# Queries and first-pair keys split once for both heads in a hybrid attention layer

## The chip, the cores and the metric

The kernel runs on one core of a Trainium2 chip. Its engines are TensorE (PE: matmuls and transposes), VectorE (DVE), ScalarE (ACT), GpSimd (POOL) and SyncE (SP), whose queue issues nearly all transfers. The metric is the device time of one execution in microseconds, the median of several runs.

## The reference

One layer over 1024 tokens of width 1024 in float32. It projects the normalised input once, and two mixers share the columns: a dilated sliding-window attention with 8 heads of 64, and a gated linear recurrence (HGRN2) with 4 heads of 128. An output projection and a squared-ReLU MLP follow.

```python
h = rmsnorm(x, mix_pre_norm[layer])
proj = h @ w_in[layer]
q_a, k_a, v_a, q_h, f_h, i_h, g_h = jnp.split(proj, splits, axis=-1)
attn = dilated_mixture_attention(q_a, k_a, v_a, slopes)   # (128,1), (512,4), (2048,16)
attn = rmsnorm(attn.reshape(B, S, ATTN_WIDTH), attn_out_norm[layer])
rec = hgrn2_recurrence(q_h, f_h, i_h, g_h, lower_bounds[layer], hgrn_out_norm[layer])
mixed = jnp.concatenate([attn, rec], axis=-1) @ w_out[layer]
x = x + rmsnorm(mixed, mix_post_norm[layer])
h = rmsnorm(x, mlp_pre_norm[layer])
ff = jnp.square(jax.nn.relu(h @ w_ff1[layer])) @ w_ff2[layer]
x = x + rmsnorm(ff, mlp_post_norm[layer])
```

In each branch of the attention the scores are `q k / 8` plus a bias that falls with distance; the three branches are combined by their softmax denominators.

## The kernel before, in words

**Precision.** A matmul in `float32r` keeps only part of a float32. So the kernel splits an operand into a high part (a copy that rounds, on ACT) and a low part (the difference, on DVE or POOL) and multiplies in three passes (`three_pass`, L89 to L92).

**Stages.** The heads of the recurrence come first: `hgrn_core(h)` for h = 0 to 3, each with projections of the next head as a filler on PE. During the core of the last head (h = 3) the filler is `attn_proj(0)` and `attn_proj(1)`, the projections of the first two pairs of attention heads. In that core each of seven levels multiplies `kt` and `qt` on DVE (L597, L599), makes the products `pl` of the next level on PE (L593) and merges them by a mask (L604). Then follow 64 steps of attention, eight per head (`s = 8 * hd + i`), with `attn_proj(2)`, `attn_proj(3)` and the first part of the output projection (`early_out`, its matmuls write `pwe`) as fillers. Then the rest of the output projection and the MLP, which are dense on PE.

**What sets the order.** The order is written out by hand and each engine takes its instructions in that order. `fill(ns)` lets the filler's generators issue a few matmuls; in a step, `UNITS[hd][i]` fills are shared between its first and its second half. `hooks[s]` is called between the two halves. `wo_half(k, c)` scales and splits half a block of the output weights (ACT L140, DVE L141), `row_turn(t, 0)` transposes four blocks of a row of the recurrence's result (PE L1174) and splits them into `emt` (ACT L86, DVE L87).

**Queries.** `attn_proj(pr)` projects a pair of heads at a time: partitions 0 to 63 of the result are the first head and 64 to 127 the second. For each half of the tokens DVE reads the bank with the factor -0.125 and the row's norm (L796) into the staging tile `qf`, in which the tokens stand by class (token mod 4). The matmul for the scores contracts over 128 partitions: a head's stack holds the query's high part in its own 64 partitions and the low part in the other 64, against keys whose high parts (`kh`) and low parts (`kl`) stand twice. So for each head ACT copies the high part into its place (L801) and POOL subtracts (L802) into the tile `ql`; SP then sends the low parts across (L803, L804).

**Keys.** `keys_read` (L731) reads a half of the keys into `kf`; `key_job` (L742) does one head of it: ACT L753, POOL L754, and two transfers (L757) to the other 64 partitions. For the first pair both jobs come at once, for later pairs one in each of several steps.

**Scores.** `look` multiplies queries and keys (PE L893, L894), and DVE adds the bias and takes the smallest value in one instruction (L898); the signs are turned, so that the smallest is the softmax's maximum. The bias tables are made by `table_part` on POOL (L718, L720) ahead of the attention. `raise_` is the exponential (ACT L951), `turn` transposes its result (`pt_D`, `pt_F`, `pt_N`: PE L961, L973, L970).

The staging tiles `half` have two buffers, which `qf`, `ql`, `kf` and the values' `vf` take in turn.

Of the kernel before, what the change touches and what calls it, by code (L numbers as in the profile page):

```python
# [9 lines left out]
F32R = mybir.dt.float32r  # L10
U8 = mybir.dt.uint8
AF = mybir.ActivationFunctionType
ALU = mybir.AluOpType
# [4 lines left out]
P = 128  # L18
# [10 lines left out]
DIL = 4  # L29
FAR = 192  # L30


def f32(ap):
    return ap.bitcast(F32)
# [3 lines left out]
def hymba_layer(ctx, tc, x, w_in, w_out, w_ff1, w_ff2, g_pre, lb_logits, g_mix, g_post,  # L38
# [21 lines left out]
    def half(name, dtype=F32):  # L60
        return sp.tile([P, 512], dtype, tag="half", name=name, bufs=2)
# [133 lines left out]
    def fill(ns, least=False):  # L195
        debt[0] += ns
        if least:
            debt[0] = max(debt[0], 1.0)
        while debt[0] > 0 and queue:
            try:  # L200
                cost = next(queue[0])
            except StopIteration:
                queue.pop(0)
                continue
            if cost is None:
                break
            debt[0] -= cost
        debt[0] = min(debt[0], 0.0)
# [191 lines left out]
    def in_blocks(ap):  # L400
        return ap.rearrange("p (j i r) -> p j r i", i=32, r=DIL)

    def classes(ap):
        return ap.rearrange("p (m r) -> p r m", r=DIL)

    def by_class(ap):
        return ap.rearrange("p (j r i) -> p j r i", i=32, r=DIL)
# [285 lines left out]
    def table_part():  # L693
        n = table_box["next"]
        hd, part_ = divmod(n, 2)
        if n > 2 * AH:
            return
        table_box["next"] += 1
        if part_ == 0 and hd > 0:
            nc.sync.dma_start(out=table_dram[hd - 1], in_=table_box["out"][:, :NEAR + FAR])  # L700
        if hd == AH:
            return
        if n == 0:
            table_box["raw"] = slab("S", "traw")
            G.memset(table_box["raw"][:, :FAR * DIL], -1.0e30)
        if part_ == 0:
            table_box["out"] = slab("S", f"tout{hd}")
        raw, dst = table_box["raw"], table_box["out"]
        w = NEAR // 2
        near_cols = bias_tab[hd][:, T - NEAR + part_ * w:T - NEAR + (part_ + 1) * w].rearrange("(i r) c -> r i c", r=DIL)  # L710
        for r in range(DIL):
            nc.sync.dma_start(out=raw[32 * r:32 * r + 32, FAR * DIL:], in_=near_cols[r])
        if part_ == 0:
            for b in range(4, NT):
                n = (b - 1) * P
                nc.sync.dma_start(out=raw[(b - 4) * 32:(b - 3) * 32, :n],
                                  in_=bias_tab[hd].rearrange("(i r) c -> i r c", r=DIL)[:, 0, 896 - b * P:896 - b * P + n])
        G.tensor_scalar(by_class(dst[:, part_ * w:(part_ + 1) * w]), in_blocks(raw[:, FAR * DIL:]), -1.0, None, op0=ALU.mult)  # L718
        if part_ == 0:
            G.tensor_scalar(dst[:, NEAR:NEAR + FAR],  # L720
                            raw[:, :FAR * DIL].rearrange("p (k r) -> p k r", r=DIL)[:, :, 0], -1.0, None, op0=ALU.mult)

    first_done = [False] * (AH // 2)
    A0 = 4 * HH
# [3 lines left out]
    turn_later = []  # L728
    second_done = [False] * (AH // 2)

    def keys_read(pr, pm, hf):  # L731
        sl = slice(hf * 512, hf * 512 + 512)
        full = half(f"kf{pr}{hf}")
        V.tensor_tensor(out=full.rearrange("p (r m) -> p r m", r=DIL), in0=classes(pm),
                        in1=rrow[:, sl].rearrange("p (r m) -> p r m", r=DIL), op=ALU.mult)
        key_jobs.extend((pr, i, hf, full) for i in range(2))
        keys_done[pr] += 1
        if pr == 0:
            key_job()
            key_job()  # L740

    def key_job():  # L742
        if not key_jobs:
            return
        pr, i, hf, full = key_jobs.pop(0)
        a, b = halves[i]

        def place_of(t):
            return t.rearrange("p (r m) -> p r m", r=DIL)[:, :, hf * P:(hf + 1) * P]
        st = pairs[pr][0][i]  # L750
        kh, kl = place_of(st["kh"]), place_of(st["kl"])
        src = full.rearrange("p (r m) -> p r m", r=DIL)[a:b]
        S.activation(kh[a:b], src, AF.Copy)  # L753
        G.tensor_tensor(out=kl[a:b], in0=src, in1=f32(kh[a:b]), op=ALU.subtract)  # L754
        c, d = halves[1 - i]
        for t in (kh, kl):
            nc.sync.dma_start(out=f32(t[c:d]), in_=f32(t[a:b]))  # L757
# [17 lines left out]
    def attn_proj(pr):  # L775
        stacks = [{}, {}]
        box = [None]
        while pr > 1 and not second_done[pr - 2]:
            yield None
        w = w_get(A0 + 3 * pr, 0)  # L780
        for hf in range(2):
            sl = slice(hf * 512, hf * 512 + 512)
            for n, cost in enumerate(proj_t(w, f"aq{pr}", hf, box)):
                if hf == 0 and n == 3 and turn_later:
                    values_turn()
                    cost += 450.0
                if hf == 0 and n == 4:
                    w_get(A0 + 3 * pr)
                if pr == 0 and hf == 0 and n == 5:
                    rrow_by_class(1)  # L790
                yield cost
            if hf == 0:
                for i in range(2):
                    stacks[i]["q"] = slab("S", f"q{pr}_{i}", F32R)
            full = half(f"qf{pr}{hf}")
            V.scalar_tensor_tensor(full.rearrange("p (r m) -> p r m", r=DIL), classes(box[0]), -0.125,  # L796
                                   rrow[:, sl].rearrange("p (r m) -> p r m", r=DIL), op0=ALU.mult, op1=ALU.mult)
            lo = half(f"ql{pr}{hf}", F32R)
            for i, (a, b) in enumerate(halves):
                src = full[a:b].rearrange("p (r j i) -> p j r i", r=DIL, i=32)  # L800
                S.activation(by_class(stacks[i]["q"][a:b, sl]), src, AF.Copy)  # L801
                G.tensor_tensor(out=by_class(lo[a:b]), in0=src, in1=by_class(f32(stacks[i]["q"][a:b, sl])), op=ALU.subtract)  # L802
            nc.sync.dma_start(out=f32(stacks[0]["q"][64:128, sl]), in_=f32(lo[0:64]))  # L803
            nc.sync.dma_start(out=f32(stacks[1]["q"][0:64, sl]), in_=f32(lo[64:128]))  # L804
            yield 650.0
        wv = w_get(A0 + 3 * pr + 1, 0)
        vs = None

        def values(hf):
            for n, cost in enumerate(proj_t(wv, f"av{pr}", hf, box)):  # L810
                if n == 4:
                    w_get(A0 + 3 * pr + 1 + hf)
                yield cost
            full = half(f"vf{pr}{hf}")
            V.tensor_tensor(out=by_class(full), in0=in_blocks(box[0]),
                            in1=rrow[:, hf * 512:hf * 512 + 512].rearrange("p (r j i) -> p j r i", r=DIL, i=32), op=ALU.mult)
            turn_later.append((pr, vs, full, hf))
            yield 650.0

        vs = slab("V8", f"v{pr}", F32R, (P, NT, 2, 2, 64))  # L820
        yield from values(0)
        while pr > 0 and not first_done[pr - 1]:
            yield None
        wk = w_get(A0 + 3 * pr + 2, 0)
        for i in range(2):
            stacks[i]["kh"] = slab("S", f"kh{pr}_{i}", F32R)
            stacks[i]["kl"] = slab("S", f"kl{pr}_{i}", F32R)
        pairs[pr] = (stacks, vs)
        for hf in range(2):
            for n, cost in enumerate(proj_t(wk, f"ak{pr}", hf, box)):  # L830
                if n == 3 and hf == 0:
                    values_turn()
                    cost += 450.0
                yield cost
            keys_read(pr, box[0], hf)
            if hf == 0 and pr == AH // 2 - 1:
                early_rows()
            yield 650.0
        yield from values(1)
# [29 lines left out]
    def look(hd, kind, g):  # L869
# [25 lines left out]
            got.append((dst, pS[:, o:o + n], bias, i))  # L895
            o += n
        for dst, src, bias, i in got:
            V.tensor_tensor_reduce(out=dst, in0=src, in1=bias, scale=1.0,  # L898
                                   scalar=3.0e38, op0=ALU.add, op1=ALU.min, accum_out=least[:, i:i + 1])

    def far_queries(hd):
# [398 lines left out]
    for h in range(HH):  # L1300
# [10 lines left out]
        1: lambda: last_gate(1),  # L1311
        2: lambda: last_gate(2),
        3: lambda: last_gate(3),
        43: lambda: wo_half(1, 0),
        45: lambda: wo_half(1, 1),
        46: lambda: [row_turn(0, 0, tag="s"), wo_half(2, 0)],
        47: lambda: [wo_half(2, 1), drain(), early_sums(), queue.extend(early_out(t) for t in range(NE))],
        48: lambda: [values_turn("t"), wo_half(3, 0)],
        49: lambda: load_bias(AH - 1),
        50: lambda: [wo_half(3, 1), row_turn(1, 0)],  # L1320
        52: lambda: row_turn(2, 0),
        54: lambda: row_turn(3, 0),
        55: lambda: [wo_half(4, 0), row_load(0)],
# [17 lines left out]
    for s in range(n_steps):  # L1341
# [46 lines left out]
        hooks.get(s, lambda: None)()  # L1388
        for _ in range(units - units // 2):
            fill(0.0, True)  # L1390
        if i in (1, 2):
            swap_low(hd, i - 1)
        if i == 7:
# [908 lines left out]
```

## Time and profile before

| | us |
|---|---|
| median of 3 runs | 1208.02 (1207.78 to 1208.76) |
| profiled execution, time | 1208.16 |
| profiled execution, span from the first to the last instruction | 1206.1 |
| PE busy | 1195.9 (99%) |
| DVE busy | 852.4 (71%) |
| ACT busy | 548.9 (46%) |
| POOL busy | 307.9 (26%) |

The granted clock of TensorE is 0.999. In the views below, a row of an engine's instructions in order of time has its start, its duration (both us), engine, line, operation, what it writes and reads, and the count of the instructions merged into it; in brackets stands the engine's idle time before it and what ended it. A row of waits has the total, the number and the longest of the waits. `xN: a/b/c` are the shortest, median and longest duration in ns. "DMA to landing" runs from an issue to the arrival of its data. PE's matmuls overlap and their ends are modelled.

### The profile page before, as it was taken

How to read it: one execution, taken by the hardware profiler on the slowest of the kernel's cores; microseconds unless marked ns; L12 is line 12 of the kernel's file. 1: busy time of each engine (PE TensorE's matmuls, PEld its weight loads, DVE VectorE, ACT ScalarE, POOL GpSimd, SP SyncE). 2: the span in 40 equal slices, each digit the busy share in tenths (PEclk: the TensorE clock that was granted, in tenths of full speed). 3: DMA queues.
4: the chain of work that ended last, by engine and by line, in shares of the span. 5: the costliest groups of instructions: out<-in, count | busy, mean ns of one | idle time of the engine just before them, and what ended most of it. 6: DMA issues, size and time to landing. Idle time of an engine off the chain costs nothing.

```text
span 1206.1 us, 17280 instructions
## 1 busy us (share of the span) xinstructions
PE 1195.9 (99%) x6342; PEld 1025.6 (85%) x6342; DVE 852.4 (71%) x1438; ACT 548.9 (46%) x1075; POOL 307.9 (26%) x290
## 2 busy tenths in 40 slices
PE   9999999999999999999999999999999999999998
PEld 8898989888888888888888888888888888888886
DVE  5696978776666768676689566766688553578796
ACT  7633333332565668755664222222234543434562
POOL 0121112021221210153321786575631000000022
PEclk9999999999999999999999999999999999999999
DMA  5222323123545456273514565554587534533337
GB/s 218 71 68 84 95 85 93 52 82 80 147 96 122 124 130 159 56 242 105 192 63 159 180 215 190 189 194 144 204 318 269 190 105 140 169 94 105 105 105 279
DMA packets 87091, 172.31 MB, mean 143 GB/s; under 512 B 14560, under 2 KB 40032, under 8 KB 87008
## 3 DMA queue, kind: packets, MB, share of 16 engines
q1 hardware_dynamic: 86864, 171.22, 44.3%
q8 instruction: 50, 0.82, 0.3%
q14 instruction: 33, 0.27, 0.1%
q10 hardware_dynamic: 144, 0.00, 0.0%
HBM read 116.91 MB, written 47.99 MB: 137 GB/s over the span
## 4 chain that ended last, share of the span: by engine, by line
PE 93%; DVE 2%; ACT 2%; issue 1%; DMA 0%; POOL 0%; DVEq 0%; POOLq 0%; ACTq 0%
PE f L2042 18%; PE f2s L2042 7%; PE pig L92 2%; PE pig L90 2%; PE pig L91 2%; PE pl L529 2%; PE pwo L90 2%; PE pwo L92 2%; PE pwo L91 2%; PE pm_ak L90 1%; PE pm_av L90 1%; PE pm_ak L92 1%; PE pm_ak L91 1%; PE pm_av L92 1%; PE pm_av L91 1%
## 5 line engine op out<-in xcount | busy, mean ns | idle before, releaser
L87 DVE TENSOR_TENSOR al<-ar,ah 128x1024 fp32r<-128x1024 f32 x56 | 70.6, 1260 | 80.5 <-ACT ah L86 78.2
L2042 PE MATMUL f<-bh,ah 128*128 128x512 f32 x320 | 124.5, 389 | 0.0
L2042 PE MATMUL f<-bl,ah 128*128 128x512 f32 x320 | 124.5, 389 | 0.0
L2042 PE MATMUL f<-bh,al 128*128 128x512 f32 x320 | 124.5, 389 | 0.0
L86 ACT ACTIVATE ah<-ar 128x1024 fp32r<-128x1024 f32 x56 | 59.1, 1056 | 86.9 <-DMA ar<-actd 83.3
L2042 PEld LDWEIGHTS f<-bh,ah 128*128 128x128 f32 x320 | 60.1, 188 | 12.6
L2042 PEld LDWEIGHTS f<-bh,al 128*128 128x128 f32 x320 | 60.1, 188 | 12.5
L2042 PEld LDWEIGHTS f<-bl,ah 128*128 128x128 f32 x320 | 60.1, 188 | 12.3
L2116 POOL TENSOR_SCALAR lbl<-ssq 128x1 f32<-128x1 f32 x4 | 3.3, 820 | 245.6 <-ACT fd L2112 245.5
L1665 POOL TENSOR_TENSOR e<-x,e 128x512 f32<-128x512 f32 x14 | 21.6, 1540 | 131.2 <-DVE x L1616 124.0
L2042 PE MATMUL f2s<-bl,ah 128*128 128x512 f32 (+1 forms) x128 | 48.9, 382 | 0.0
L2042 PE MATMUL f2s<-bh,al 128*128 128x512 f32 (+1 forms) x128 | 48.9, 382 | 0.0
L2042 PE MATMUL f2s<-bh,ah 128*128 128x512 f32 (+1 forms) x128 | 48.9, 382 | 0.0
L718 POOL TENSOR_SCALAR tout<-traw 128x256 f32<-128x256 f32 x16 | 18.4, 1149 | 109.2 <-DMA traw<-in_bias_tab_dram 93.4
L754 POOL TENSOR_TENSOR kl<-kf,kh 64x512 fp32r<-64x512 f32 x16 | 21.3, 1329 | 86.3 <-ACT kh L753 55.6
L87 DVE TENSOR_TENSOR bl<-br,bh 128x1024 fp32r<-128x1024 f32 x32 | 40.1, 1252 | 1.1 <-ACT bh L86 0.9
L2059 ACT ACTIVATE acc<-f 128x512 f32<-128x512 f32 x28 | 16.8, 598 | 49.6 <-PE f L2042 49.6
L802 POOL TENSOR_TENSOR ql<-qf,q 64x512 fp32r<-64x512 f32 x16 | 21.3, 1334 | 62.6 <-ACT q L801 62.0
L86 ACT ACTIVATE bh<-br 128x1024 fp32r<-128x1024 f32 x32 | 33.6, 1051 | 4.4 <-PE f L2042 3.1
L87 DVE TENSOR_TENSOR wl<-raw,wh 128x1024 fp32r<-128x1024 f32 x21 | 25.9, 1233 | 9.3 <-ACT wh L86 9.3
L90 PE MATMUL pwo<-woh,mt 128*128 128x512 f32 x80 | 32.2, 402 | 0.0
L92 PE MATMUL pwo<-woh,mt 128*128 128x512 f32 x80 | 31.3, 391 | 0.0
(1722 smaller groups left out, 3964.2 us busy)
## 6 DMA issues: line engine op xcount, KB each, us to landing
ar<-actd SPq DMA_DIRECT2D x56, 512.0 KB, 3.7
br<-in_w_ff_dram SPq DMA_DIRECT2D x16, 1024.0 KB, 6.2
raw<-in_w_in_dram SPq DMA_DIRECT2D x28, 512.0 KB, 4.0
w1r<-in_w_ff_dram SPq DMA_DIRECT2D x14, 1024.0 KB, 6.5
actd<-e SPq DMA_DIRECT2D x17, 768.0 KB, 4.3
actd<-e SPq DMA_DIRECT2D x11, 1024.0 KB, 4.1
xr<-in_x_dram SPq DMA_DIRECT2D x8, 512.0 KB, 8.3
raw<-in_w_out_dram SPq DMA_DIRECT2D x8, 512.0 KB, 3.6
```

The lines of the kernel that those rows point to most:

```text
L86: S.activation(hi, src, AF.Copy)
L87: eng.tensor_tensor(out=lo, in0=src, in1=f32(hi), op=ALU.subtract)
L90: TE.matmul(dst, lhs[0], rhs[0], start=start, stop=False)
L91: TE.matmul(dst, lhs[0], rhs[1], start=False, stop=False)
L92: TE.matmul(dst, lhs[1], rhs[0], start=False, stop=stop)
L529: TE.matmul(pl[:, n % 2, :192], kt[:, n * P:(n + 1) * P], sets[u // 2][:, n % 4], start=True, stop=True)
L718: G.tensor_scalar(by_class(dst[:, part_ * w:(part_ + 1) * w]), in_blocks(raw[:, FAR * DIL:]), -1.0, None, op0=ALU.mult)
L754: G.tensor_tensor(out=kl[a:b], in0=src, in1=f32(kh[a:b]), op=ALU.subtract)
L802: G.tensor_tensor(out=by_class(lo[a:b]), in0=src, in1=by_class(f32(stacks[i]["q"][a:b, sl])), op=ALU.subtract)
L1665: eng[0].tensor_tensor(out=e1[:, 3], in0=a21, in1=e1[:, 2], op=ALU.add)
L2042: TE.matmul(pm, a[:, j, c], b[:, j, d], start=start and j == 0 and q == 0, stop=stop and j == 1 and q == 2, skip_group_check=True)
L2059: S.activation(acc_at(p, i), pm, AF.Copy)
```

## The change

The split is made once for 128 partitions, that is for both heads: `both_parts` copies the high part into a second staging tile and subtracts in place, so that the first tile becomes the low part. For the queries of every pair and for the keys of the first pair, SP then sends high and low parts to their places: four transfers per query half (two before) and eight per first-pair key half (four before). Later pairs' keys go on by `key_job`. The query's read takes the order of blocks that the values' read has and leaves out the factor; the scores' read scales by -0.125, and the bias tables carry 8 for -1. `wo_half(1, 0)` goes from step 43 to 44, and `row_turn(1, 0)` from the middle of step 50 to behind its second fill.

```diff
-        G.tensor_scalar(by_class(dst[:, part_ * w:(part_ + 1) * w]), in_blocks(raw[:, FAR * DIL:]), -1.0, None, op0=ALU.mult)
+        G.tensor_scalar(by_class(dst[:, part_ * w:(part_ + 1) * w]), in_blocks(raw[:, FAR * DIL:]), 8.0, None, op0=ALU.mult)
...
+    def both_parts(full, name):
+        hi = half(f"hi{name}", F32R)
+        S.activation(hi, f32(full), AF.Copy)
+        G.tensor_tensor(out=full, in0=f32(full), in1=f32(hi), op=ALU.subtract)
+        return hi, full
...
-        full = half(f"kf{pr}{hf}")
+        full = half(f"kf{pr}{hf}", F32R)
...
-        key_jobs.extend((pr, i, hf, full) for i in range(2))
         keys_done[pr] += 1
-        if pr == 0:
-            key_job()
-            key_job()
+        if pr > 0:
+            key_jobs.extend((pr, i, hf, full) for i in range(2))
+            return
+        for q, src in zip(("kh", "kl"), both_parts(full, f"k{pr}{hf}")):
+            for i, (a, b) in enumerate(halves):
+                dst = f32(pairs[pr][0][i][q]).rearrange("p (r m) -> p r m", r=DIL)[:, :, hf * P:(hf + 1) * P]
+                for c, d in halves:
+                    nc.sync.dma_start(out=dst[c:d], in_=f32(src[a:b]).rearrange("p (r m) -> p r m", r=DIL))
...
-            full = half(f"qf{pr}{hf}")
-            V.scalar_tensor_tensor(full.rearrange("p (r m) -> p r m", r=DIL), classes(box[0]), -0.125,
-                                   rrow[:, sl].rearrange("p (r m) -> p r m", r=DIL), op0=ALU.mult, op1=ALU.mult)
-            lo = half(f"ql{pr}{hf}", F32R)
+            full = half(f"qf{pr}{hf}", F32R)
+            V.tensor_tensor(out=by_class(f32(full)), in0=in_blocks(box[0]),
+                            in1=rrow[:, sl].rearrange("p (r j i) -> p j r i", r=DIL, i=32), op=ALU.mult)
+            hi, lo = both_parts(full, f"q{pr}{hf}")
             for i, (a, b) in enumerate(halves):
-                src = full[a:b].rearrange("p (r j i) -> p j r i", r=DIL, i=32)
-                S.activation(by_class(stacks[i]["q"][a:b, sl]), src, AF.Copy)
-                G.tensor_tensor(out=by_class(lo[a:b]), in0=src, in1=by_class(f32(stacks[i]["q"][a:b, sl])), op=ALU.subtract)
-            nc.sync.dma_start(out=f32(stacks[0]["q"][64:128, sl]), in_=f32(lo[0:64]))
-            nc.sync.dma_start(out=f32(stacks[1]["q"][0:64, sl]), in_=f32(lo[64:128]))
+                c, d = halves[1 - i]
+                nc.sync.dma_start(out=f32(stacks[i]["q"][a:b, sl]), in_=f32(hi[a:b]))
+                nc.sync.dma_start(out=f32(stacks[i]["q"][c:d, sl]), in_=f32(lo[a:b]))
...
-            V.tensor_tensor_reduce(out=dst, in0=src, in1=bias, scale=1.0,
+            V.tensor_tensor_reduce(out=dst, in0=src, in1=bias, scale=-0.125,
...
-        43: lambda: wo_half(1, 0),
+        44: lambda: wo_half(1, 0),
...
-        50: lambda: [wo_half(3, 1), row_turn(1, 0)],
+        50: lambda: wo_half(3, 1),
...
         for _ in range(units - units // 2):
             fill(0.0, True)
+        if s == 50:
+            row_turn(1, 0)
```

More of the change, by code (lines that the diff above doesn't have):

```diff
@@ L717, in table_part @@
                                   in_=bias_tab[hd].rearrange("(i r) c -> i r c", r=DIL)[:, 0, 896 - b * P:896 - b * P + n])
-        G.tensor_scalar(by_class(dst[:, part_ * w:(part_ + 1) * w]), in_blocks(raw[:, FAR * DIL:]), -1.0, None, op0=ALU.mult)
+        G.tensor_scalar(by_class(dst[:, part_ * w:(part_ + 1) * w]), in_blocks(raw[:, FAR * DIL:]), 8.0, None, op0=ALU.mult)
         if part_ == 0:
             G.tensor_scalar(dst[:, NEAR:NEAR + FAR],
-                            raw[:, :FAR * DIL].rearrange("p (k r) -> p k r", r=DIL)[:, :, 0], -1.0, None, op0=ALU.mult)
+                            raw[:, :FAR * DIL].rearrange("p (k r) -> p k r", r=DIL)[:, :, 0], 8.0, None, op0=ALU.mult)
     first_done = [False] * (AH // 2)
@@ L729, in hymba_layer @@
     second_done = [False] * (AH // 2)
+    def both_parts(full, name):
[3 more added lines that the diff above has]
+        return hi, full
     def keys_read(pr, pm, hf):
         sl = slice(hf * 512, hf * 512 + 512)
-        full = half(f"kf{pr}{hf}")
-        V.tensor_tensor(out=full.rearrange("p (r m) -> p r m", r=DIL), in0=classes(pm),
+        full = half(f"kf{pr}{hf}", F32R)
+        V.tensor_tensor(out=f32(full).rearrange("p (r m) -> p r m", r=DIL), in0=classes(pm),
                         in1=rrow[:, sl].rearrange("p (r m) -> p r m", r=DIL), op=ALU.mult)
-        key_jobs.extend((pr, i, hf, full) for i in range(2))
         keys_done[pr] += 1
-        if pr == 0:
-            key_job()
-            key_job()
+        if pr > 0:
[6 more added lines that the diff above has]
+                    nc.sync.dma_start(out=dst[c:d], in_=f32(src[a:b]).rearrange("p (r m) -> p r m", r=DIL))
     def key_job():
@@ L751, in key_job @@
         kh, kl = place_of(st["kh"]), place_of(st["kl"])
-        src = full.rearrange("p (r m) -> p r m", r=DIL)[a:b]
+        src = f32(full).rearrange("p (r m) -> p r m", r=DIL)[a:b]
         S.activation(kh[a:b], src, AF.Copy)
```

## The prediction, as recorded before the change was run

> **What bounds the kernel now.** I read the page first, then the waits of the tensor engine, then its instructions in order of time around each wait, and then the other engines' instructions in the same stretch.
>
> ```profile
> PE 1195.9 (99%) x6342; PEld 1025.6 (85%) x6342; DVE 852.4 (71%) x1438; ACT 548.9 (46%) x1075; POOL 307.9 (26%) x290
> PE pl L593 <- DVE tot L603: 0.6, 1, 0.6
> ...
> PE pmt L1174 <- DVE ptl L991: 0.5, 1, 0.5
> PE pt_F L973 <- ACT pf L951: 0.5, 1, 0.5
> PE pd L1044 <- DVE stat L898: 0.2, 1, 0.2
> PE pov_far L1031 <- DVE ptNl L991: 0.2, 1, 0.2
> ```
>
> PE is busy for 1195.9 of 1206.1 us, and all that the change edits runs on ACT, POOL, DVE and SP. So the work that it saves there is worth nothing by itself: it can only pay where PE waits for one of them. The list of PE's waits is short, and in the attention's stretch it holds four or five single waits. Its figures are too small, because a matmul's end is modelled: it lasts 0.39 us in the rows, but the next one starts 0.23 us after it. I therefore measure a stall from start to start.
>
> ```profile
> 257.83 0.39 PE L92 MATMUL pm_av<-hTh,wl 128*128 128x512 f32 x1
> 258.36 1.89 PE L593 MATMUL pl<-qt,kt 128*128 128x64 f32 x15
> ...
> 278.18 0.39 PE L92 MATMUL pm_ak<-hTh,wl 128*128 128x512 f32 x1
> 279.19 1.08 PE L593 MATMUL pl<-qt,kt 128*128 128x64 f32 x8 [0.62 <-DVE tot L603]
> ...
> 454.08 0.27 PE L973 MATMUL pt_F<-ident,pf 128*128 128x128 f32 x1
> 454.88 0.44 PE L973 MATMUL pt_F<-ident,pf 128*128 128x128 f32 x2 [0.53 <-ACT pf L951]
> ...
> 457.39 0.62 PE L970 MATMUL pt_N<-ident,pn 128*128 128x128 f32 x4
> ...
> 472.05 0.62 PE L1090 MATMUL pot<-ident,o 128*128 128x128 f32 x4
> 473.22 0.66 PE L1174 MATMUL pmt<-ident,erows 128*128 128x128 f32 x4 [0.55 <-DVE ptl L991]
> ```
>
> Stall 1: the matmul at 257.83 should be followed at 258.06, and is at 258.36: 0.30 us. Stall 2: 278.41 against 279.19, 0.78 us. Transposes follow each other by (0.62 - 0.27) / 3 = 0.12 us. Stall 3: 454.20 against 454.88, 0.68 us. Stall 4: 472.05 + 4 x 0.12 = 472.53 against 473.22, 0.69 us. Together 2.45 us. What is left in the waits' list of this stretch is the two entries of 0.2 us, each some 0.15 us more from start to start by the same reckoning, so 0.7 us. About 3.2 us is thus the most that any edit here can win before the MLP.
>
> **The change, part by part.**
>
> *The split of both heads at once.* Two ACT copies and two POOL subtractions of 64 partitions become one of each of 128, for eight query halves and for two key halves of the first pair.
>
> ```profile
> L802 POOL TENSOR_TENSOR ql<-qf,q x16: 1275/1290/1627, 254.8 to 426.1; 64x512 fp32r<-64x512 f32 x16
> L1665 POOL TENSOR_TENSOR e<-x,e 128x512 f32<-128x512 f32 x14 | 21.6, 1540 | 131.2 <-DVE x L1616 124.0
> L801 ACT ACTIVATE q<-qf x16: 627/632/634, 254.1 to 424.7; 64x512 fp32r<-64x512 f32 x16
> ```
>
> POOL takes about as long for 128 partitions (1540 ns) as for 64 (1290 to 1627). ACT should too: its scaled copy of 128 x 512 (L140, quoted below) holds it 0.61 us, the one of 64 x 512 takes 0.63. Each half saves one ACT copy (10 x 0.63 = 6.3 us in all) and one POOL subtraction (10 x 1.3 to 1.5). Of this only what touches stalls 1 and 2 counts. There POOL slows DVE:
>
> ```profile
> 271.26 0.69 DVE L597 TENSOR_TENSOR kt<-kt,tot 128x512 f32<-128x512 f32 x1 [0.41 <-PE pl L593]
> 261.16 0.67 DVE L599 TENSOR_TENSOR qt<-qt,tot 128x512 f32<-128x512 f32 x1
> 275.82 1.52 DVE L597 TENSOR_TENSOR kt<-kt,tot 128x512 f32<-128x512 f32 x1 [1.04 <-PE pl L593]
> 277.26 1.78 DVE L599 TENSOR_TENSOR qt<-qt,tot 128x512 f32<-128x512 f32 x1
> 275.52 2.98 POOL L754 TENSOR_TENSOR kl<-kf,kh 64x512 fp32r<-64x512 f32 x2 [11.10 <-ACT kh L753]
> ...
> 256.52 1.78 DVE L599 TENSOR_TENSOR qt<-qt,tot 128x512 f32<-128x512 f32 x1
> 254.77 2.98 POOL L802 TENSOR_TENSOR ql<-qf,q 64x512 fp32r<-64x512 f32 x2 [11.02 <-ACT q L801]
> ```
>
> The same two operations take 0.69 and 0.67 us with POOL idle, and 1.52 and 1.78 us while POOL subtracts. With one subtraction POOL is done at 275.52 + 1.5 = 277.0. The first operation then ends where it did, at 277.34, and the second runs alone, to 277.26 + 0.67 = 277.93 instead of 279.04. PE follows it by 0.15 us (279.19 - 279.04), so it could start at 278.08, ahead of the 278.41 at which it arrives: stall 2 goes whole, 0.78 us, with 0.3 us to spare. At stall 1 POOL runs from 254.77 to 257.75; with one subtraction it is done at 256.3, before the second operation starts at 256.52, and this ends at 257.2 instead of 258.30: stall 1 goes, 0.30 us. Bounds: nothing (if the slow operations have another cause) to 1.08 us. I take 1.08. The page "SBUF — State Buffer" of the Trainium skill (section "Who interferes with whom") says that a DVE instruction with two SBUF inputs and a GpSimd one that reads SBUF exclude each other, the later one blocking until the other is finished; by that the first operation would wait for 277.0 and end at 277.7, the second at 278.4, and 0.1 us of stall 2 would be left. The rows agree that they hinder each other, but 277.34 is too early for a full block.
>
> *Transfers.* The high part is no longer written in place by ACT but sent.
>
> ```profile
> L803 SPq DMA_DIRECT2D q<-ql x8: 461/498/552, 256.1 to 426.0; - x8
> L757 SPq DMA_DIRECT2D kh<-kh x16: 590/591/647, 275.5 to 461.3; - x16
> DMA to landing us min/median/max: 2.2/2.3/5.4
> kh<-kh SPq DMA_DIRECT2D x16, 128.0 KB, 2.4
> SPq L803 <- POOL ql L802: 20.5, 8, 6.8
> L894 PE MATMUL ps_D<-kl,q x32: 273/313/401, 302.4 to 491.6; 128*128 128x128 f32 x8, 128*128 128x256 f32 x8, 128*128 128x384 f32 x8, 128*128 128x512 f32 x8
> ```
>
> SP issues 2 more per query half (16 x 0.50 = 8 us) and 4 more per first-pair key half (8 x 0.59 = 4.7 us). SP already stands 20.5 us waiting for POOL's low parts, which now come a subtraction (1.3 us) sooner; the two more issues (1.0 us) fit in that. The last keys of the first pair: the second read ends near 284.7, ACT at 285.4, four issues until 287.8, four more until 290.2, landed 2.4 us later at 292.6; their first reader is at 302.4. Queries of later pairs are read a whole pair later. Cost 0. Without that cover each chain would be about 2.9 us longer (0.5 to issue, 2.4 to land).
>
> *Tiles held longer.* The staging tiles have two buffers, and a query's whole value becomes its own low part in place: the next half's read (on DVE) must wait for landings, where it waited for POOL. At the tightest place the low parts are issued until about 257.85 (POOL done at 256.3, three issues of 0.5) and land at 259.7; the read stood at 259.92. Behind it on DVE are the next level's two operations, for which PE waits. I take 0, with up to 0.2 us late; the next `pl` has cover.
>
> *Reads and factors.* The query's read becomes a plain product in the values' layout (0.69 us) for the one with a factor (0.71 in the row at 259.92, below); the factor 8 in the tables and -0.125 in the scores' read change constants alone. Cost 0; no row has other constants, and I see nothing for either sign beyond the spread of these rows.
>
> ```profile
> L815 DVE TENSOR_TENSOR vf<-pm_av,rrow x8: 679/691/693, 267.6 to 463.1; 128x512 f32<-128x512 f32 x8
> ```
>
> *`wo_half(1, 0)` from step 43 to 44.*
>
> ```profile
> 452.40 0.71 ACT L140 ACTIVATE woh<-raw,gcols 128x512 fp32r<-128x512 f32 x1
> 453.01 0.44 ACT L951 ACTIVATE pf<-pf,stat 128x192 f32<-128x192 f32 x1
> ...
> 457.01 0.19 ACT L951 ACTIVATION_READ_ACCUMULATOR pn<-pn,stat 128x1 f32 x1
> ```
>
> It takes 0.61 us of ACT (453.01 - 452.40) ahead of the exponentials. The one that PE waits for ends 0.61 us sooner, and PE goes on at 454.27 instead of 454.88: 0.61 of stall 3's 0.68 us. But in step 44 the same 0.61 us stand ahead of the next exponentials, so these still end at 457.20. PE would come to `pt_N` at 456.78, to its third transpose at 457.02, and wait until 457.25 (PE follows ACT by 0.05, as at 454.88). This gives 0.24 back: 0.37 us net, between 0 and 0.68.
>
> *`row_turn(1, 0)` behind the fill of step 50.*
>
> ```profile
> 473.92 0.60 ACT L86 ACTIVATE emt<-pmt 128x512 fp32r<-128x512 f32 x1 [0.61 <-PE pmt L1174]
> 474.62 0.60 ACT L1196 ACTIVATE esum<-pwe 128x512 f32<-128x512 f32 x1
> ```
>
> PE does three matmuls (0.7 us) while DVE frees the bank, and comes to the transposes at 473.2, when it is free: stall 4 goes, 0.69 us. What is late next is ACT, which in the old order first waits for these transposes (from 473.92) and then takes `esum`; now it takes `esum` about 0.5 us sooner and then the transposes' split, so it is ahead by about as much as PE. I take 0.67, bounds 0 and 0.69.
>
> **Sum.** 0.30 + 0.78 + 0.37 + 0.67 = 2.12 us. Everything after 515 us is PE at its pace and moves as a block. The profiled execution took 1208.16 us (span 1206.1), the runs' median is 1208.02; 1208.16 - 2.1 = 1206.0 against the one, 1205.9 against the other, which I forecast. This is 0.18%, and a difference of 0.2% (2.4 us) is about what a measurement of this kernel can tell from no change.
>
> **Rivals.**
>
> *A: nothing is given back, or the small waits go too.* All four stalls whole are 2.45 us, with the two small ones 3.2: 1204.8 to 1205.6. For it speaks that ACT is freer by a copy per half; against it, that the small waits hang on DVE's work behind PE in a stretch that the change leaves as it is.
>
> *B: POOL is not what slows DVE.* Then stalls 1 and 2 stay and 1.04 us is won: 1207.0. With both moves taken back as well it would be no change. Against it speak the rows at 271.26 and 275.82, the same line and shape, with POOL idle and busy.
>
> *C, slower: the query's read waits for landings.*
>
> ```profile
> 259.92 0.71 DVE L796 SCALAR_TENSOR_TENSOR qf<-pm_aq,rrow 128x512 f32<-128x512 f32 x1
> ...
> 263.69 0.89 PE L593 MATMUL pl<-qt,kt 128*128 128x64 f32 x7
> ...
> q<-ql SPq DMA_DIRECT2D x2, 128.0 KB, 5.1
> ```
>
> Between 306 and 314 us the same transfer took 5.1 us. If it did so at 259.92, the read would come at 257.4 + 5.1 = 262.5, 2.6 us late. PE's next `pl` is at 263.69 and the operation whose result it needs (the row at 261.16 above) ends at 261.83, so 1.9 us are covered and 0.7 lost. To end 2.4 us above 1208.0 the loss must be 4.5 us, a landing of 8.9 us there; the slowest seen is 5.4.
>
> **How the numbers follow.** Forecast (1.6 to 2.4 us won) 0.48; A 0.36; B and what lies down to no gain 0.10; C 0.06. Faster by over 0.2% is A, 0.36; the forecast and B are within 0.2%, 0.58; slower 0.06. The range 1204.7 to 1207.8 takes in A's best and B's 1207.0 with some loss of C, and leaves out about 0.12. The forecast's own range is 1205.6 to 1206.4.
>
> **What would show it.** Right: no wait of PE's `pl` at L593 for DVE; one POOL subtraction of about 1.5 us per query half, and `qt` at 0.7 us behind it; no wait of `pmt` after `pot`; a `pt_F` wait under 0.1 us, with a new one of 0.2 us at `pt_N`. Wrong: DVE's query reads idle for a landing; POOL at 2.5 us or more for 128 partitions (stall 2 would stay); or new PE waits in the steps after 42, where ACT is nearly full.

## The result, and the profile after

| | before | changed |
|---|---|---|
| median of 15 runs each, us | 1207.95 (1207.78 to 1208.76) | 1205.53 (1205.39 to 1205.71) |
| profiled execution, time / span, us | 1208.16 / 1206.1 | 1205.52 / 1203.5 |
| busy us: PE, DVE, ACT, POOL | 1195.9, 852.4, 548.9, 307.9 | 1195.3, 849.7, 542.3, 294.7 |

The changed kernel is 2.42 us faster, a ratio of 0.998 with a 95% interval of 0.9973 to 0.9987. That is 0.20%, on the line that the prediction drew between a gain and no change. The forecast was 1205.9 us. The measured time lies inside the range of 1204.7 to 1207.8, but 0.07 us below the forecast's own range (1205.6 to 1206.4), in the stretch that the prediction gave to rival A. The waits below tell the two apart.

The waits of the tensor engine in the changed kernel (engine and line, what it waited for: us in total, times, longest):

```profile
PE pig L310 <- DVE zero L231: 1.0, 1, 1.0
PE pig L322 <- ACT wig0h L86: 0.3, 1, 0.3
PE pd L1052 <- DVE stat L906: 0.2, 1, 0.2
PE ps_N L901 <- DVE stat L906: 0.2, 1, 0.2
PE xt L286 <- DMA xr<-in_x_dram: 0.2, 1, 0.2
PE pov_far L1039 <- DVE ptNl L999: 0.2, 1, 0.2
```

The waits of `pl`, `pmt` and `pt_F` are gone. One is new: `ps_N` for DVE's scores' read. The two small ones, `pd` and `pov_far`, are still there. The wait of the first transposes for the input is 0.2 us where it was 0.6 (0.3 in a second profile of the changed kernel). No edit is ahead of it, so I take it for a difference between executions; the profiled execution of before was also 0.2 us above its kernel's median. It is taken out below.

PE's instructions in order of time at the four places, and at the two where something was expected to be late next (lines have moved: the tables' L973 is L981, L970 is L978, L893 is L901, L1174 is L1182; a row's count stops where the stretch that was asked for ends, so `pl` has fewer than its 16):

```profile
257.47 0.39 PE L92 MATMUL pm_av<-hTh,wl 128*128 128x512 f32 x1
257.70 1.56 PE L593 MATMUL pl<-qt,kt 128*128 128x64 f32 x13
...
277.43 0.39 PE L92 MATMUL pm_ak<-hTh,wl 128*128 128x512 f32 x1
277.65 1.11 PE L593 MATMUL pl<-qt,kt 128*128 128x64 f32 x9
...
452.38 0.63 PE L981 MATMUL pt_F<-ident,pf 128*128 128x128 f32 x3
...
455.08 0.90 PE L978 MATMUL pt_N<-ident,pn 128*128 128x128 f32 x4
...
463.46 0.39 PE L901 MATMUL ps_N<-kh,q 128*128 128x256 f32 x1 [0.19 <-DVE stat L906]
...
471.36 0.66 PE L1182 MATMUL pmt<-ident,erows 128*128 128x128 f32 x4
```

Both `pl` now start 0.22 to 0.23 us after the matmul before them, so without a stall. The three `pt_F`, the first of which stood 0.8 us ahead of the other two, are through in 0.63 us. `pt_N` takes 0.90 us for four transposes that took 0.62.

The same matmul's start in the two profiles gives PE's lead, and each step of it one term of the sum. Ahead of the first place the lead is 0.35 to 0.41 us, the start's. Then:

| place | lead after it, us | step | predicted |
|---|---|---|---|
| stall 1, first `pl` | 0.66 to 0.77 | +0.3 to 0.4 | +0.30 |
| stall 2, second `pl` | 1.54 to 1.61 | +0.8 | +0.78 |
| state update `pu` (before: 292.83) | 1.73 | +0.1 | none |
| stall 3, `pt_F` | 2.32 | +0.59 | +0.61 |
| `pt_N` | 2.03 to 2.09 | -0.2 to -0.3 | -0.24 |
| `ps_N` (before: 465.17) | 1.71 | -0.3 to -0.4 | none |
| far scores `ps_F` (before: 470.09) | 1.84 | +0.14 | none |
| stall 4, `pmt` | 2.51 to 2.56 | +0.7 | +0.67 |

Without the start that is 2.2 us, against 2.12 forecast; the medians differ by 2.42. At 535 us the lead is still 2.56: the rest of the kernel moves as a block.

DVE and POOL at the first two places, first of before (POOL, which the prediction showed with its two subtractions merged into one row), then of the changed kernel:

```profile
275.52 1.27 POOL L754 TENSOR_TENSOR kl<-kf,kh 64x512 fp32r<-64x512 f32 x1 [11.10 <-ACT kh L753]
...
276.87 1.63 POOL L754 TENSOR_TENSOR kl<-kf,kh 64x512 fp32r<-64x512 f32 x1
```

```profile
274.81 1.29 POOL L734 TENSOR_TENSOR kf<-kf,hik 128x512 fp32r<-128x512 f32 x1 [13.33 <-ACT hik L733]
...
275.06 1.58 DVE L597 TENSOR_TENSOR kt<-kt,tot 128x512 f32<-128x512 f32 x1 [1.04 <-PE pl L593]
276.57 0.68 DVE L599 TENSOR_TENSOR qt<-qt,tot 128x512 f32<-128x512 f32 x1
...
254.72 1.53 DVE L597 TENSOR_TENSOR kt<-kt,tot 128x512 f32<-128x512 f32 x1
256.17 0.68 DVE L599 TENSOR_TENSOR qt<-qt,tot 128x512 f32<-128x512 f32 x1
```

One subtraction, one slow product, and the second at 0.68 us, as predicted. At the second query half it is `qt` that is slow (1.79 us from 260.24, beside POOL's 1.36 us from 260.12); PE does not wait there.

### The profile page after: what moved, and what is told of

Same layout as the page of the kernel before. It is cut to its first block, busy times and chain, and to the rows that moved or that the text cites. A ratio compares the mean times of both kernels' runs of the same rounds, so it can differ in the third digit from the quotient of the medians.

```text
span 1203.5 us, 17310 instructions
## 1 busy us (share of the span) xinstructions
PE 1195.3 (99%) x6342; PEld 1025.7 (85%) x6342; DVE 849.7 (71%) x1438; ACT 542.3 (45%) x1065; POOL 294.7 (24%) x280
## 4 chain that ended last, share of the span: by engine, by line
PE 96%; ACT 2%; DVE 1%; issue 1%; DMA 0%; POOL 0%; DVEq 0%; POOLq 0%; ACTq 0%
PE f L2052 18%; PE f2s L2052 7%; PE pig L92 2%; PE pig L90 2%; PE pig L91 2%; PE pl L529 2%; PE pwo L90 2%; PE pwo L92 2%; PE pwo L91 2%; PE pm_ak L90 1%; PE pm_aq L90 1%; PE pm_f L90 1%; PE pm_aq L92 1%; PE pm_ak L92 1%; PE pm_ak L91 1%; PE pm_aq L91 1%
## 5 line engine op out<-in xcount | busy, mean ns | idle before, releaser
L764 POOL TENSOR_TENSOR kl<-kf,kh 64x512 fp32r<-64x512 f32 x12 | 15.4, 1287 | 70.9 <-ACT kh L763 49.4
L91 PE MATMUL pwo<-wol,mt 128*128 128x512 f32 x80 | 31.2, 390 | 0.0
```

The lines of the kernel that those rows point to most:

```text
L91: TE.matmul(dst, lhs[0], rhs[1], start=False, stop=False)
```

## The experiments

Times are medians of 11 runs, each beside the kernel before on the same chip. That stood at 1207.88 us for the first four, 1207.91 for the next four, 1207.91 for the last two. The changed kernel, run again with the second four, had 1205.62.

**The changed kernel again**, as the measure for the edits made to it:

> The changed kernel unaltered, beside the others on the same chip: 1205.5 within 0.15 us. It shows what of a difference of 0.2 to 0.4 us is the chip's and the start's.

1205.62 us; ratio to before 0.9984 (0.9975 to 0.9992), 2.29 us faster than before. Seven of the eleven times are 1205.4 to 1205.6 and four are 1206.6 to 1207.1; nothing here shows why. The 15 of the first measurement lie within 0.32 us. In its profile PE's lead over before starts at 0.21 us and is 2.47 us behind `pmt`, so the steps make 2.26 where the first profile had 2.2: they hold in both.

**The moves alone.** To the kernel before:

```diff
-        43: lambda: wo_half(1, 0),
+        44: lambda: wo_half(1, 0),
-        50: lambda: [wo_half(3, 1), row_turn(1, 0)],
+        50: lambda: wo_half(3, 1),
...
+        if s == 50:
+            row_turn(1, 0)
```

> The kernel before with the two moves alone (wo_half(1, 0) to step 44, row_turn(1, 0) behind step 50's fills). Theory: the moves act by themselves. The turn's move clears PE's wait of 0.69 us at pmt; the other clears 0.6 us at pt_F and gives it back at pt_N (0.24) and at the next ps_N (0.39). Stalls 1 and 2 (PE's pl for DVE, 0.30 and 0.78 us) stay. About 0.7 us faster than before: 1207.2. Rival: the moves only pay together with the new split, which frees ACT and POOL; then it stands within 0.3 us of before, 1208.

1207.03 us, 0.85 faster than before; ratio 0.9994 (0.9985 to 1.0003). The list of PE's waits:

```profile
PE pl L593 <- DVE tot L603: 0.6, 1, 0.6
...
PE ps_N L893 <- DVE stat L898: 0.2, 1, 0.2
```

The second `pl` still waits, and the new wait at `ps_N` is there without the new split, so it belongs to the moves. PE's lead goes 0.37 (start), 0.98 at `pt_F`, 0.69 at `pt_N`, 0.37 at `ps_N`, 0.51 at `ps_F`, and 1.23 behind `pmt`: at `ps_N` the gain of the first move is used up.

**The split alone.** Both moves undone in the changed kernel.

> The changed kernel with both moves undone. Theory: stalls 1 and 2 are gone, the stalls at pt_F (0.7 us) and pmt (0.7 us) are back; 1.1 to 1.5 us faster than before, 1206.5 to 1206.9. Rival (the moves do it all): the time of before, 1207.9.

1206.40 us, 1.48 faster than before; ratio 0.9989 (0.998 to 0.9998). The old waits of `pmt` and `pt_F` (0.5 us each in the list) are back, `ps_N`'s is not there. 0.85 and 1.48 make 2.33, within 0.1 us of both measurements of the whole gain (2.42 and 2.29): to that accuracy the two parts act by themselves.

**POOL at work for longer.** In the changed kernel:

```diff
         G.tensor_tensor(out=full, in0=f32(full), in1=f32(hi), op=ALU.subtract)
+        G.tensor_tensor(out=full, in0=f32(full), in1=f32(ones).to_broadcast([P, 512]), op=ALU.mult)
```

> The changed kernel, with a second POOL operation of 128 x 512 behind each subtraction (it multiplies the low part by one), so that POOL is as long at work as before while ACT, DVE, SP and the transfers are as in the changed kernel. Theory (POOL slows DVE's products of two SBUF operands): kt and qt are at 1.5 and 1.8 us again behind the first pair's queries and keys, and PE waits again at the two pl, 0.3 and 0.8 us: 1.1 us slower than the changed kernel, 1206.6. Rival (the gain there came from something else, ACT's or the transfers' new order): qt stays at 0.7 us and the time at 1205.5.

1206.88 us, 1.3 us slower than the changed kernel; ratio to before 0.9993 (0.9984 to 1.0002). POOL and DVE at the second place, then DVE's read of the second query half, then PE at the second `pl`:

```profile
275.03 1.28 POOL L734 TENSOR_TENSOR kf<-kf,hik 128x512 fp32r<-128x512 f32 x1 [10.76 <-ACT hik L733]
276.39 1.37 POOL L735 TENSOR_TENSOR kf<-kf,ones 128x512 fp32r<-128x512 f32 x1
...
275.27 1.59 DVE L597 TENSOR_TENSOR kt<-kt,tot 128x512 f32<-128x512 f32 x1 [0.98 <-PE pl L593]
276.79 1.52 DVE L599 TENSOR_TENSOR qt<-qt,tot 128x512 f32<-128x512 f32 x1
...
260.04 0.69 DVE L807 TENSOR_TENSOR qf<-pm_aq,rrow 128x512 f32<-128x512 f32 x1 [0.63 <-DMA q<-hiq]
...
277.64 0.39 PE L92 MATMUL pm_ak<-hTh,wl 128*128 128x512 f32 x1
278.46 1.97 PE L593 MATMUL pl<-qt,kt 128*128 128x64 f32 x16 [0.44 <-DVE tot L603]
```

Only POOL's work was added, and `qt` is slow again (1.52 us for 0.68), and PE waits 0.6 us at the second `pl`, from start to start. So the gain of the split at stall 2 is POOL's absence. Stall 1 came back by some 0.15 us of PE's lead and not by the 0.3 expected: POOL's two operations took 2.74 us together, from 254.30 to 257.04, where the two subtractions of before took 2.98, so `qt` was through sooner. Against the changed kernel PE's lead falls by 0.7 us at stall 2, 0.15 at stall 1 and 0.1 each at 268 and 501 us; the rest of the 1.3 us stays open. DVE's row at 260.04 is the rival of the staging tiles in small: the longer chain on POOL makes the transfers late, and DVE's read stands 0.63 us for a landing.

**The subtraction on DVE.**

```diff
-        G.tensor_tensor(out=full, in0=f32(full), in1=f32(hi), op=ALU.subtract)
+        V.tensor_tensor(out=full, in0=f32(full), in1=f32(hi), op=ALU.subtract)
```

> The changed kernel with the subtraction on DVE in place of POOL. Theory: kt and qt run at 0.7 us, since POOL is idle beside them; DVE has ten more operations of 0.7 us and waits for ACT ahead of each, which the pl of the recurrence's last head can afford: stalls 1 and 2 stay away, time as the changed kernel's within 0.3 us, 1205.3 to 1205.8. Rival: the wait for ACT on DVE's queue (0.7 us for each) comes out at PE in the attention's steps, some 1 to 2 us slower, 1206.5 to 1207.5.

1207.88 us: all of the gain is gone (ratio to before 1.0, 0.9991 to 1.0009). DVE's rows, and PE's waits:

```profile
275.67 0.68 DVE L597 TENSOR_TENSOR kt<-kt,tot 128x512 f32<-128x512 f32 x1
276.27 0.68 DVE L599 TENSOR_TENSOR qt<-qt,tot 128x512 f32<-128x512 f32 x1
...
304.32 0.69 DVE L734 TENSOR_TENSOR qf<-qf,hiq 128x512 fp32r<-128x512 f32 x1 [0.75 <-ACT hiq L733]
```

```profile
PE ps_N L901 <- DVE stat L906: 1.3, 3, 0.6
...
PE pot L1098 <- DVE anat L1102: 0.6, 1, 0.6
```

With POOL idle both products run at 0.68 us (at the first place, 0.69 us each from 256.46), and stalls 1 and 2 stay away, so POOL's share in stall 1 is shown here. But in the attention DVE stands 0.75 us for ACT with the scores' reads queued behind, and PE waits for these and once for `anat`. That is the rival's mechanism, at a higher price than I gave it (1206.5 to 1207.5). The subtraction is dear on the engine whose queue PE waits for; on POOL none of PE's waits in the changed kernel comes from it.

**`wo_half(1, 0)` back at step 43** in the changed kernel.

> The changed kernel with wo_half(1, 0) back at step 43. Theory as the prediction had it: 0.37 us slower than the changed kernel. Theory as the trace of the changed kernel suggests (ACT is full until DVE's next free time, so the 0.6 us won at pt_F are lost again at pt_N and ps_N): pt_F waits 0.7 us again, the waits at pt_N (0.2) and ps_N (0.35) are gone, and the time is that of the changed kernel within 0.15 us.

1205.63 us against 1205.62: no difference. The list has `pt_F` again, and no `ps_N`:

```profile
PE pt_F L981 <- ACT pf L959: 0.5, 1, 0.5
```

ACT and DVE ahead of and behind the moved work, first in the changed kernel, then with the work at 43:

```profile
450.17 0.62 ACT L763 ACTIVATE kh<-kf 64x512 fp32r<-64x512 f32 x1
454.06 0.36 ACT L991 ACTIVATE ptFh<-pt_F 128x256 fp32r<-128x256 f32 x1
462.98 0.42 DVE L906 CUSTOM_DVE_ANT_0 pn<-ps_N,bt 128x256 f32<-128x256 f32 x1
...
450.26 0.62 ACT L763 ACTIVATE kh<-kf 64x512 fp32r<-64x512 f32 x1
454.15 0.36 ACT L991 ACTIVATE ptFh<-pt_F 128x256 fp32r<-128x256 f32 x1
463.07 0.42 DVE L906 CUSTOM_DVE_ANT_0 pn<-ps_N,bt 128x256 f32<-128x256 f32 x1
```

The two executions stand 0.09 us apart ahead of the moved work and 0.09 us apart behind it. ACT is full there, so the order of its work changes nothing for what follows, down to the read that `ps_N` waits for (the last row, done at 463.40; `ps_N` starts at 463.46).

**`row_turn(1, 0)` back in step 50's middle.**

> The changed kernel with row_turn(1, 0) back in the middle of step 50. Theory: PE waits 0.7 us at pmt for the bank and nothing later gives it back: 0.7 us slower than the changed kernel. Rival (ACT is full behind it too and takes part of the gain back): 0.3 to 0.5 us slower.

1206.27 us, 0.65 slower than the changed kernel. Only the wait at `pmt` (0.69 us by the prediction's reckoning) is back, and PE's lead falls by 0.66 us there. That bears out the difference against the spread of the changed kernel's times. This move keeps its gain.

**All keys split at once**, for every pair right behind the read:

```diff
-        if pr > 0:
-            key_jobs.extend((pr, i, hf, full) for i in range(2))
-            return
```

> The changed kernel with every pair's keys split at once for both heads, no key jobs. Theory (ACT is the bound between 453 and 461 us): ACT loses a copy of 0.63 us in that stretch, so the waits at pt_N (0.2) and ps_N (0.35) shrink or go: 0.3 to 0.6 us faster than the changed kernel. Rival: eight transfers of 0.6 us in a row stand in SP's queue ahead of the weights' loads and the sums that are sent for the joint softmax, or a key's slot is not yet free and all behind it on SP waits: 1 us or more slower.

1206.27 us, 0.65 slower than the changed kernel. ACT, then PE:

```profile
449.36 0.63 ACT L733 ACTIVATE hik<-kf 128x512 fp32r<-128x512 f32 x1 [1.84 <-DVE kf L740]
```

```profile
450.48 0.33 PE L978 MATMUL pt_F<-ident,pf 128*128 128x128 f32 x1
451.40 0.44 PE L978 MATMUL pt_F<-ident,pf 128*128 128x128 f32 x2 [0.59 <-ACT pf L956]
```

The wait at `ps_N` is gone, as expected of a freer ACT. But the copy now stands in ACT's queue ahead of the exponentials and waits 1.84 us for the read: PE loses 0.81 us at `pt_F`. So the theory missed, and the loss is not the rival's either: PE waits for ACT, not for a transfer.

**All keys split once, but later**, at the place of the next key job, and at the latest ahead of the next read of keys or values:

```diff
         sl = slice(hf * 512, hf * 512 + 512)
+        key_job()
...
-        if pr > 0:
-            key_jobs.extend((pr, i, hf, full) for i in range(2))
+        key_jobs.append((pr, hf, full))
+        if pr == 0:
+            key_job()
+
+    def key_job():
+        if not key_jobs:
             return
+        pr, hf, full = key_jobs.pop(0)
         for q, src in zip(("kh", "kl"), both_parts(full, f"k{pr}{hf}")):
...
+            key_job()
             full = half(f"vf{pr}{hf}")
```

> The changed kernel with every pair's keys split once for both heads, but for later pairs at the place of the first key job after the read, not right behind the read. Theory (in the kernel with all keys split at once PE's new wait of 0.8 us at pt_F came from ACT standing for the keys' read with exponentials queued behind it): that wait goes, and ACT's two copies of 0.63 us less between 447 and 461 us also take away the waits at pt_N (0.2) and ps_N (0.35): 0.3 to 0.6 us faster than the changed kernel, 1205.0 to 1205.3. Rival (eight transfers of 0.6 us in a row on SP are what costs): 1206.2 as with all keys at once.

1207.22 us, 1.6 slower than the changed kernel. The theory missed what the copy needs besides its input:

```profile
451.90 0.63 ACT L733 ACTIVATE hik<-kf 128x512 fp32r<-128x512 f32 x1 [1.57 <-DMA kl<-kf]
...
443.56 2.62 SPq L756 DMA_DIRECT2D kh<-hik  x4
446.28 2.60 SPq L756 DMA_DIRECT2D kl<-kf  x4
```

```profile
453.02 0.33 PE L971 MATMUL pt_F<-ident,pf 128*128 128x128 f32 x1 [0.42 <-ACT pf L949]
454.30 0.44 PE L971 MATMUL pt_F<-ident,pf 128*128 128x128 f32 x2 [0.96 <-ACT pf L949]
```

ACT waits 1.57 us for the landing of the other half's last transfer, whose staging tile the copy takes over. That half's eight transfers hold SP from 443.56 to 448.88 us, so the expectation's rival, eight in a row, has its part in how late that landing is. This is rival C of the prediction with keys in the queries' place, and PE pays 1.7 us at `pt_F`. A third staging tile was not tried.

**The same with `wo_half(1, 0)` at 43.**

> The same with wo_half(1, 0) back at step 43. Theory: pt_F waits 0.6 to 0.7 us again, and with ACT freer behind it nothing gives that back: 0.3 to 0.6 us slower than with it at 44. Rival (the place of wo_half is worth nothing whatever else ACT has to do): the same time as with it at 44.

1209.27 us, but 1207.53 to 1211.06, so the median says little. Four runs with a mean granted clock of 0.999 to 1.000 took 1207.5 to 1208.0 us; seven with 0.996 to 0.998 took 1209.1 to 1211.1. The profiled run is one of the seven and lost ground in two ways. PE waits 1.27 and 1.17 us at `pt_F`, and then its clock drops (window in us, then PE, PEld, DVE, ACT and POOL busy, granted clock, DMA share and GB/s):

```profile
452.00:456.00 4.00, 1.94 (x10) 1.18 (x9) 2.16 (x4) 3.91 (x13) 1.27 (x1) 1.00 0.59 133
456.00:457.00 1.00, 1.00 (x7) 1.00 (x6) 0.27 (x1) 0.96 (x4) 0.00 (x0) 0.54 1.00 202
457.00:458.00 1.00, 1.00 (x4) 0.85 (x4) 0.91 (x4) 1.00 (x4) 0.00 (x0) 0.50 0.97 181
458.00:459.00 1.00, 1.00 (x5) 0.86 (x4) 0.97 (x2) 0.43 (x2) 0.00 (x0) 0.50 1.00 201
```

Here the place of `wo_half` is worth 0.7 us at the first `pt_F` (a stall of 1.27 us against 0.59), and the four runs at the full clock are 0.3 to 0.8 us above the 1207.22 with it at 44, about as expected. So the move is worth something once ACT has less to do behind it; in the changed kernel it is not.

## Why the prediction was right, and where its steps were not

- *Only PE's waits count.* Right. ACT lost 6.6 us of work and POOL 13.2, and the time moved by 2.4 us, by what came off PE's waits less what came back.
- *Stalls 1 and 2 go because POOL subtracts once.* Right, 1.1 to 1.2 us for 1.08, and shown: with POOL's work added back stall 2 returned, and with the subtraction on DVE, and POOL idle, both stalls stayed away. One reading in it was wrong. I held that 277.34 was too early for the full block that the Trainium skill's page "SBUF — State Buffer" (section "Who interferes with whom") describes, because I gave POOL's first subtraction 1.5 us, half of a merged row. It took 1.27 and ended at 276.79; the product ended 0.55 us behind. In the changed kernel (276.10 and 276.64) and with POOL's second operation (276.31 and 276.86, then 277.76 and 278.31) it is 0.54 to 0.55 us again, for a product that takes 0.68 alone: it gets hardly anything done until POOL is through. These rows agree with that rule, and the sum is the same by it, since POOL needs 1.29 us for 128 partitions and not the 1.5 that I took from another operation.
- *The turn's move.* Right, 0.7 us in the profile and 0.65 undone alone, for 0.67.
- *`wo_half`'s move, 0.37 us net.* This is the term that was mis-sized: it is worth nothing here (1205.63 against 1205.62). The first two steps were as written (0.59 won at `pt_F`, 0.2 to 0.3 back at `pt_N`). I stopped there. But in the changed kernel ACT has no gap from 450.17 to 461.70. DVE stands for ACT's `emt` at 459.01 and is full from there to the scores' read that frees the bank of `ps_N`, so that read is no sooner than with the work at 43: 0.3 to 0.4 us more are given back. What I should have done is to follow the full engines to their next idle time before pricing the move.
- *Transfers, staging tiles, reads, factors: 0.* Right in the changed kernel: no query's read on DVE waited for a landing. But the cover is thin. With a longer chain on POOL a read waited 0.63 us, and with all keys by this way PE lost 1.7 us.
- *Left over.* `pu` and `ps_F` gave 0.1 us each that I had not seen, which made up for most of `wo_half`. So it is partly luck that the sum came out within 0.4 us: one term was nothing, and two small ones were missing. The time falls in rival A's stretch, but not for A's reason, as `pt_N` and `ps_N` gave back and the two small waits stayed. Between the 2.2 us of the profiles and the 2.42 of the medians, 0.2 us stays open; the start alone varies by that much.

## What to carry to other kernels

Where one engine is 99% busy, list its waits, measure each from start to start, and cost an edit by the waits that it touches; work saved elsewhere counts for nothing. A stall that is removed by moving work later on a full engine may be no gain, so follow that engine, and those that wait for it, to the next gap before pricing the move. When a copy in place becomes a staging tile and a transfer, the landing decides when the tile is free, and whichever in-order engine writes the tile next waits with all its queue behind it.

## What the runs showed of the hardware

- POOL took as long for 64 partitions by 512 (1.27 us alone) as for 128 (1.28 to 1.30), so joining two heads in one subtraction halved its time.
- DVE's product of two SBUF operands that starts under a POOL subtraction ends 0.54 to 0.56 us behind it; and the POOL subtraction that started while such a product was running (276.87, the product until 277.34) took 1.63 us instead of 1.27.
- In the profiled run of the last experiment two PE waits of 1.27 and 1.17 us with one transpose (0.1 us) between were followed by some 3 us at a granted clock of 0.50 to 0.54; waits of 0.59 and 1.17 us at the same place in the run before it were not. Over it PE lost about 1.4 us of its lead (from -0.30 to -1.73). Four of that kernel's eleven runs have the mean clock of the other kernels (0.999 to 1.000) and are over 1 us faster than the seven others, so the drop seems not to come every time; there is no trace of these four.
